# A 14th weight unit in the ring of an expert layer, with one buffer of turned rows and one-hot lists of two experts

## The chip, the cores and the metric

The kernel runs on one core of a Trainium2 chip. Its time is the device time of one execution in microseconds (us). The shapes are fixed: 512 tokens of width 1024, two layers, float32 in and out.

## What is computed

Each of the two layers mixes the tokens (three kinds of attention behind one input projection and one output projection) and then sends every token to 2 of 32 experts. The part that matters here is the second:

```python
def hier_moe(x, rg_w, rg_b, re_w, re_b, w_gate, w_up, w_down):
    t = x.reshape(B * S, D)                       # 512 x 1024
    lg = einsum('td,dg->tg', t, rg_w) + rg_b      # 4 groups
    g_star = argmax(lg, -1)                       # the best group
    le = ...                                      # its 8 experts' logits
    top_v, top_i = lax.top_k(le, 2)               # two experts
    gate = ...                                    # their weights
    for g in range(4):
        h = silu(t @ w_gate[g]) * (t @ w_up[g])   # 1024 -> 256, each of 8 experts
        y = y + (h * gate) @ w_down[g]            # 256 -> 1024
    return y

for l in range(2):
    x = layer_norm(ALPHA * x + hybrid_mixer(x, ...))
    x = layer_norm(ALPHA * x + hier_moe(x, ...))
```

An expert's weights (gate, up, down) are 3 x 1024 x 256 float32 numbers, 3 MB; 32 experts make 96 MB in each layer, read once.

## The kernel before

**Experts.** The kernel does two experts at a time: 16 steps `p` in a layer, and each expert has room for 64 tokens, so a step has 128 rows. For step `p` it gathers 128 rows of the normalised tokens from HBM (`fetch`, `gathered`: an indirect DMA on POOL's queue from `xd` into a part of `xroom`), transposes and scales them (`turned`: 8 PE transposes, then ACT and DVE write `xg`), multiplies by gate and up (`experts_up`, 32 matmuls into `S`), applies silu (`experts_mid`), transposes `h` and multiplies by down (`experts_down`, 16 matmuls into `o`), adds the rows' own share (`half_rows` made it: two DVE operations over 128 x 1024) and scatters the result to `y2` with another indirect DMA. `lists(b)` makes the row numbers and weights of four experts, that is of two steps: DVE compares positions with slots (`hots`, the one-hot matrix `oneh`), PE multiplies it with a table of tokens, and a few small DVE operations turn that into row numbers (`slot_rows`). `oneh` has one buffer.

**The ring of weights.** An expert's 3 MB are two units of 128 x 3072 float32 (1536 KB): `u` = 0 holds gate and up for k = 0 to 5, `u` = 1 the rest of them and down. A layer loads 64 units in a fixed order (both experts' `u` = 0, then both experts' `u` = 1). Each goes into the next place of a ring that is written out as a string, one letter a place:

```python
RING = "UUAAARTTXUUmm"
...
EW.setdefault(e, {})[u] = unit(RING[(2 * j + d) % len(RING)], "w")
SP.dma_start(EW[e][u][:, c0:c1], a["w_e"][l, e, u, :, c0:c1])
```

The letters name memory that the attention part uses for something else: U four slots of projection weights, A three work areas, R the landing area of raw weights, X a part of `xroom` (free when the output projection has read its input there), T and m units of the pool that replaces attention's tiles (`moe`). 13 letters make 13 units of room: unit n + 13 can be loaded when unit n has been read for the last time. `load_next(n)` emits n pairs of units: one pair before attention's softmax part, two within the output projection, three when the pool `moe` opens, and then two pairs in every step, one after `experts_up` and one after `experts_down`. Loads are issued by SP, in order; each waits at SP until its room is free. A scheduler at compile time orders each engine's instructions by their place in the program and by when it thinks they are ready, so a load whose room is free earlier can stand in SP's queue ahead of one that was emitted before it.

**The end of a layer.** At step 13 the first half of the result (`yf`) is read back into two units (one m, one A), at the end the second half and the norm's rows (`yt`, two A units). The next layer's first projection weights are loaded through the landing area R (`raw_room`, `load_pair`: SP loads, ACT and DVE or POOL split into two parts).

Of the kernel before, what the change touches and what calls it, by code (L numbers as in the profile page):

```python
# [7 lines left out]
F32 = mybir.dt.float32  # L8
F32R = mybir.dt.float32r
# [3 lines left out]
OP = mybir.AluOpType  # L13
# [3 lines left out]
NT = S // 128  # L17
NK = D // 128
# [6 lines left out]
NE, FH, CAP = 32, 256, 64  # L25
# [39 lines left out]
def trunk(tc, a, out, dbg=None):  # L65
# [4 lines left out]
    with es:  # L70
# [9 lines left out]
        def bank(tag):  # L80
            return ps.tile([128, 512], F32, name=tag, tag=tag)
# [14 lines left out]
        def mm(o, l, r, start, stop):  # L96
            return PE.matmul(o, l, r, start=start, stop=stop, skip_group_check=True)  # L97
# [10 lines left out]
        def cc(name):  # L108
            return cst[:, CO[name][0] - KEPT:CO[name][1] - KEPT]
# [60 lines left out]
        RAW = {}  # L170

        def raw_room():
            RAW[0] = raws.tile([128, UNIT], F32, name="raw", tag="raw")
# [74 lines left out]
        for l in range(DEPTH):  # L248
# [40 lines left out]
            def load(c):  # L289
                if c < 9:  # L290
                    Wc[l, c] = load_pair(w_in_src(l, c), chunks[c][1])
# [12 lines left out]
                return [x[:, i, c0:c1] for i in range(NT)]  # L304


            load(2)
            if l == 0:
                setup()
# [115 lines left out]
            t = bank("T")  # L425
# [84 lines left out]
            def unit(kind, name):  # L510

                if kind == "X":
                    return xroom[:, 0:UNIT]
                pool, tag, bufs = dict(U=(slots, "U", 4), A=(ums, "Um", 3), R=(raws, "raw", 1), m=(units["m"], "m", 2), T=(units["m"], "T", 2))[kind]
                return pool.tile([128, UNIT], F32, name=name, tag=tag, bufs=bufs)

            RING = "UUAAARTTXUUmm"

            def load_next(n=1):

# [495 lines left out]

            def turned(xr):

                xg = mo.tile([128, NK, 128], F32, name="xg", tag="xg", bufs=2)
                for h in range(2):  # L1020
                    t = bank("acc")
                    for j in range(4):
                        k = 4 * h + j
                        PE.transpose(t[:, 128 * j:128 * j + 128], xr[:, 128 * k:128 * k + 128], ident)  # L1024
                    for j in range(4):
                        k, o = 4 * h + j, t[:, 128 * j:128 * j + 128]
                        if h:
                            A.activation(xg[:, k], o, AF.Identity, scale=lv[:, 0, k, 0:1], bias=lv[:, 0, k, 1:2])  # L1028
                        else:
                            V.tensor_scalar(xg[:, k], o, lv[:, 0, k, 0:1], lv[:, 0, k, 1:2], op0=OP.mult, op1=OP.add)  # L1030
                return xg
# [43 lines left out]

            RI, XR, XG, HR = {}, {}, {}, {}

            def hots(b):
                P = cp.tile([128, NT, 4, CAP], F32R, name="oneh", tag="oneh")
                for i in range(NT):  # L1080
                    last_on["hot"] = V.tensor_tensor(P[:, i], posm[:, i, 4 * b:4 * b + 4].unsqueeze(2).to_broadcast([128, 4, CAP]),
                                    cc("slot")[:, 0:CAP].unsqueeze(1).to_broadcast([128, 4, CAP]), OP.is_equal)
                return P

            def lists(b, P=None):

                Pf = (P or hots(b)).rearrange("p t e s -> p t (e s)")
                for q in range(2):
                    t = bank("T")
                    e0 = 4 * b + 2 * q  # L1090
                    for i in range(NT):
                        mm(t[:, 0:6], Pf[:, i, 128 * q:128 * q + 128], tok[:, i, :, e0:e0 + 2], i == 0, i == NT - 1)
                    rv = small.tile([128, 3], F32, name="rv", tag="rv", bufs=8)
                    V.tensor_copy(rv[0:64], t[0:64, 0:6:2])
                    V.tensor_copy(rv[64:128], t[64:128, 1:6:2])
                    RI[2 * b + q] = slot_rows(rv)
# [30 lines left out]
            attn.__exit__(None, None, None)  # L1127
            moe = tc.tile_pool(name=f"moe{l}", bufs=1, reuse_waits="tile")
            mo = units["m"] = moe.__enter__()
            load_next(3)  # L1130
            XG[0], HR[0] = turned(XR[0]), half_rows(XR.pop(0))
            lists(1)
            fetch(2)
# [29 lines left out]
            def overflow():  # L1163

                n_items = nc.values_load(eidi[0:1, MAX_ITEMS:MAX_ITEMS + 1], min_val=0, max_val=MAX_ITEMS)
                with tc.For_i(0, n_items) as item:
# [43 lines left out]
                    t = bank("acc")  # L1210
                    for k in range(NK):
                        PE.transpose(t[:, 64 * k:64 * k + 64], xr[0:64, 128 * k:128 * k + 128], ident[0:64, 0:64])
                    xg = mo.tile([128, NK, CAP], F32, name="xg", tag="xg", bufs=2)
                    gb = [lv[:, 0, :, b:b + 1].to_broadcast([128, NK, CAP]) for b in range(2)]
                    V.tensor_tensor(xg, t.rearrange("p (k s) -> p k s", k=NK), gb[0], OP.mult)
                    V.tensor_tensor(xg, xg, gb[1], OP.add)
# [23 lines left out]
            for p in range(NE // 2):  # L1240
# [15 lines left out]
                sts.append(st)  # L1256
                if p == NE // 2 - 3:

                    for j, u in enumerate((unit("m", "yf"), unit("A", "yf"))):
                        yf = carve(u, 0, [2, D])  # L1260
                        for i in range(2):
                            yfs.append(yf[:, i])
                            r = 256 * j + 128 * i
                            firsts.append(SP.dma_start(yf[:, i], y2[r:r + 128, :]))
# [7 lines left out]
                SP.dma_start(gb2[j], a["ln_rows"][l:l + 1, 1, j].to_broadcast([128, D]))  # L1272
            with tc.issue_after(last_on["PE"].ins), tc.issue_after(last_on["V"].ins), tc.issue_after(st.ins):
                if not last:
                    raw_room()
                    Wc[l + 1, 0] = load_pair(w_in_src(l + 1, 0), chunks[0][1], "VG")
            overflow()

# [107 lines left out]
```

## Time and profile before

| | |
|---|---|
| time, median of 3 runs | 1354.07 us (1353.26 to 1357.51) |
| the profiled execution | 1356.09 us, span 1354.3 us |
| mean granted clock of TensorE | 0.948 |
| PE busy | 1172.7 us (87%) |
| DVE busy | 794.8 us (59%) |
| q1 (SP's loads), share of 16 DMA engines | 53.6% of the span |
| HBM read | 282.26 MB |

The span is the time from the first to the last instruction. PE is TensorE (PEld its weight loads), DVE VectorE, ACT ScalarE, POOL GpSimd, and SP the engine that issues most of the DMAs (SPq is its queue of instructions, POOLq and ACTq those of POOL and ACT). L530 is line 530 of the kernel above. A busy share is an average over stages with different limits. In the two expert stages (from about 405 to 637 us and from about 1059 to 1289 us) the weights come from HBM. DMA is the mean busy share of 16 DMA engines.

### The profile page before, as it was taken

What the parts mean: (1) busy time and instruction counts of PE and PEld (TensorE: products, weight loads), DVE (VectorE), ACT (ScalarE), POOL (GpSimd) and SP (SyncE); (2) the same over time, 40 slices, a digit from 0 to 9 for tenths busy, and PEclk for the clock granted to TensorE, in tenths of its full rate; (3) what the DMA queues carried; (4) which work ended last, traced back from release to release, by engine and by line L of the source; (5) the groups of instructions that cost most, each with busy time, mean ns of one, the idle gap of its engine ahead of it and who ended that gap; (6) DMA issues with size and microseconds to landing.
All of it is one profiled execution on the core that took longest, in us unless ns stands there. A gap on an engine that the chain in (4) does not pass through costs nothing. (4 is left out here: it accounts for less than half of the span.)

```text
span 1354.3 us, 18414 instructions
## 1 busy us (share of the span) xinstructions
PE 1172.7 (87%) x6708; PEld 819.8 (61%) x6708; DVE 794.8 (59%) x2007; ACT 424.7 (31%) x1019; POOL 301.4 (22%) x310
## 2 busy tenths in 40 slices
PE   6989999999969999777599899999998799988830
PEld 6989986668944444232498899666697343333310
DVE  6599638675355745332768992667635465533336
ACT  3462247574112111111236322857711111111100
POOL 5322431300111211100542434230011121111013
PEclk9999999999979999989699999899999799999975
DMA  6452440005188999999542524200335899999933
GB/s 237 115 182 82 125 171 12 22 15 218 63 366 321 424 422 423 425 407 339 194 145 74 198 75 135 104 23 23 131 135 235 317 422 424 423 425 420 392 138 125
DMA packets 68317, 302.21 MB, mean 223 GB/s; under 512 B 16128, under 2 KB 20736, under 8 KB 52864
## 3 DMA queue, kind: packets, MB, share of 16 engines
q1 hardware_dynamic: 57696, 280.02, 53.6%
q0 software_dynamic: 9376, 16.80, 3.3%
q10 hardware_dynamic: 1152, 4.19, 0.8%
q8 instruction: 54, 0.88, 0.3%
q14 instruction: 39, 0.32, 0.1%
HBM read 282.26 MB, written 36.01 MB: 235 GB/s over the span
## 5 line engine op out<-in xcount | busy, mean ns | idle before, releaser
L97 PE MATMUL acc<-U,xh 128*128 128x384 f32 (+1 forms) x1584 | 297.7, 342 | 17.4 <-ACT U L196 7.2
L97 PE MATMUL S<-w,xg 128*64 128x512 f32 (+1 forms) x968 | 265.4, 601 | 31.0 <-DMA w<-w_e 18.5
L97 PEld LDWEIGHTS acc<-U,xh 128*128 128x128 f32 x1584 | 279.8, 193 | 20.2 <-ACT U L196 7.4
L97 PEld LDWEIGHTS S<-w,xg 128*64 128x64 f32 x968 | 88.4, 140 | 155.1 <-issue 103.0
L97 PE MATMUL o<-w,hT 128*64 128x512 f32 x488 | 124.7, 597 | 8.3 <-DVE hT L92 4.4
L199 POOL TENSOR_TENSOR U<-raw,U 128x768 fp32r<-128x768 f32 (+2 forms) x46 | 92.2, 2010 | 176.1 <-ACT U L196 169.3
L1057 ACT ACTIVATE h<-S 128x256 f32<-128x256 f32 x32 | 12.3, 384 | 357.1 <-PE S L97 357.1
L1058 DVE TENSOR_TENSOR h<-h,S 128x256 f32<-128x256 f32 x32 | 13.4, 420 | 175.2 <-ACT h L1057 175.1
L1013 POOL DMA_INDIRECT xroom<-xd,ri x33 | 40.7, 1232 | 261.2 <-issue 193.3
L196 ACT ACTIVATE U<-raw 128x768 fp32r<-128x768 f32 (+2 forms) x88 | 68.2, 812 | 83.0 <-PE acc L97 42.0
L97 PEld LDWEIGHTS o<-w,hT 128*64 128x64 f32 x488 | 40.8, 136 | 72.0 <-issue 49.9
L199 DVE TENSOR_TENSOR U<-raw,U 128x768 fp32r<-128x768 f32 (+2 forms) x42 | 51.5, 1227 | 42.1 <-ACT U L196 39.5
L1072 DVE SCALAR_TENSOR_TENSOR xroom<-o,rv,xroom 128x512 f32<-128x512 f32 x64 | 47.8, 750 | 42.7 <-PE o L97 39.5
L1073 POOL DMA_INDIRECT y<-xroom,ri x32 | 32.7, 1022 | 170.3 <-DVE xroom L1072 146.5
L1028 ACT ACTIVATE xg<-acc,lv 128x128 f32<-128x128 f32 x128 | 48.1, 456 | 57.1 <-PE acc L1024 55.9
L90 ACT ACTIVATE uc<-T 128x512 f32<-128x512 f32 (+3 forms) x117 | 51.4, 461 | 40.6 <-PE T L297 38.5
L97 PE MATMUL acc<-U,oh 128*128 128x384 f32 (+1 forms) x384 | 63.3, 315 | 0.0
L97 PEld LDWEIGHTS acc<-U,oh 128*128 128x128 f32 x384 | 56.8, 189 | 1.2 <-issue 1.0
L1024 PEld LDWEIGHTS acc<-cst,xroom 128*128 128x128 f32 x256 | 29.7, 149 | 38.2 <-issue 25.9
L1036 DVE TENSOR_TENSOR xroom<-xroom,gb 128x1024 f32<-128x1024 f32 (+1 forms) x33 | 40.2, 1219 | 20.1 <-DMA xroom<-xd,ri 20.0
L403 DVE MATCH_REPLACE8 uc<-m,uc 128x256 f32<-128x256 f32 (+2 forms) x96 | 51.4, 540 | 0.0
L1030 DVE TENSOR_SCALAR xg<-acc,lv 128x128 f32<-128x128 f32 x128 | 43.6, 402 | 12.6 <-PE acc L1024 12.6
(377 smaller groups left out, 2034.5 us busy)
## 6 DMA issues: line engine op xcount, KB each, us to landing
w<-w_e SPq DMA_DIRECT2D x110, 1536.0 KB, 26.0
raw<-w_in SPq DMA_DIRECT2D x64, 384.0 KB, 3.6
xroom<-w_e SPq DMA_DIRECT2D x8, 1536.0 KB, 25.8
w<-w_e SPq DMA_DIRECT2D x24, 512.0 KB, 15.1
y<-uc SPq DMA_DIRECT2D x2, 4096.0 KB, 14.2
raw<-w_o SPq DMA_DIRECT2D x16, 384.0 KB, 3.5
xd<-yn ACTq DMA_DIRECT2D x8, 512.0 KB, 6.8
yf<-y SPq DMA_DIRECT2D x8, 512.0 KB, 11.2
```

The source lines that it names most:

```text
L90: A.activation(o, i, AF.Copy, scale=1.0 if scale is None else scale)
L97: return PE.matmul(o, l, r, start=start, stop=stop, skip_group_check=True)
L196: A.activation(hi, r, AF.Copy)
L199: e.tensor_tensor(lo, r, hi.bitcast(F32), OP.subtract)
L403: V.match_replace(out=acc_t[i][:, :n], in_to_replace=m8, in_values=acc_t[i][:, :n], imm_value=TAKEN)
L1013: G.indirect_dma_start(out=xr[0:n], out_offset=None, in_=xd, in_offset=bass.IndirectOffsetOnAxis(ap=ri[0:n], axis=0), bounds_check=S - 1, ...
L1024: PE.transpose(t[:, 128 * j:128 * j + 128], xr[:, 128 * k:128 * k + 128], ident)
L1028: A.activation(xg[:, k], o, AF.Identity, scale=lv[:, 0, k, 0:1], bias=lv[:, 0, k, 1:2])
L1030: V.tensor_scalar(xg[:, k], o, lv[:, 0, k, 0:1], lv[:, 0, k, 1:2], op0=OP.mult, op1=OP.add)
L1036: V.tensor_tensor(y[0:n], xr[0:n], gb1[0:n, 0], OP.mult)
L1072: last_on["V"] = V.scalar_tensor_tensor(y[:, c], o[n], rows[1], y[:, c], op0=OP.mult, op1=OP.add)
L1073: return G.indirect_dma_start(out=y2, out_offset=bass.IndirectOffsetOnAxis(ap=rows[2], axis=0), in_=y, in_offset=None, bounds_check=2 * S ...
```

## The change

A 14th place in the ring, a third `m` unit, and the units in another order: X and one U now come ahead of T T, three m behind them, and a U stands last. Four pairs instead of three are emitted when `moe` opens, so that 14 units are emitted ahead of step 0 instead of 12. For the room, `xg` has one buffer instead of two, and `oneh` holds two experts instead of four: `hots` is called twice in `lists`, with one buffer, so its second call must wait until PE has read the first. `yf` goes into two m units, and the next layer's first raw weights into an m unit instead of R; R is taken again when the next layer loads its third piece (`load(2)`).

```diff
@@ -304,6 +304,8 @@
                 return [x[:, i, c0:c1] for i in range(NT)]
 
 
+            if l:
+                raw_room()
             load(2)
             if l == 0:
                 setup()
@@ -511,10 +513,10 @@
 
                 if kind == "X":
                     return xroom[:, 0:UNIT]
-                pool, tag, bufs = dict(U=(slots, "U", 4), A=(ums, "Um", 3), R=(raws, "raw", 1), m=(units["m"], "m", 2), T=(units["m"], "T", 2))[kind]
+                pool, tag, bufs = dict(U=(slots, "U", 4), A=(ums, "Um", 3), R=(raws, "raw", 1), m=(units["m"], "m", 3), T=(units["m"], "T", 2))[kind]
                 return pool.tile([128, UNIT], F32, name=name, tag=tag, bufs=bufs)
 
-            RING = "UUAAARTTXUUmm"
+            RING = "UUAAARXUTTmmmU"
 
             def load_next(n=1):
 
@@ -1016,7 +1018,7 @@
 
             def turned(xr):
 
-                xg = mo.tile([128, NK, 128], F32, name="xg", tag="xg", bufs=2)
+                xg = mo.tile([128, NK, 128], F32, name="xg", tag="xg", bufs=1)
                 for h in range(2):
                     t = bank("acc")
                     for j in range(4):
@@ -1075,21 +1077,21 @@
 
             RI, XR, XG, HR = {}, {}, {}, {}
 
-            def hots(b):
-                P = cp.tile([128, NT, 4, CAP], F32R, name="oneh", tag="oneh")
+            def hots(p):
+                P = cp.tile([128, NT, 2, CAP], F32R, name="oneh", tag="oneh")
                 for i in range(NT):
-                    last_on["hot"] = V.tensor_tensor(P[:, i], posm[:, i, 4 * b:4 * b + 4].unsqueeze(2).to_broadcast([128, 4, CAP]),
-                                    cc("slot")[:, 0:CAP].unsqueeze(1).to_broadcast([128, 4, CAP]), OP.is_equal)
+                    last_on["hot"] = V.tensor_tensor(P[:, i], posm[:, i, 2 * p:2 * p + 2].unsqueeze(2).to_broadcast([128, 2, CAP]),
+                                    cc("slot")[:, 0:CAP].unsqueeze(1).to_broadcast([128, 2, CAP]), OP.is_equal)
                 return P
 
             def lists(b, P=None):
 
-                Pf = (P or hots(b)).rearrange("p t e s -> p t (e s)")
                 for q in range(2):
+                    Pf = (hots(2 * b + q) if q or P is None else P).rearrange("p t e s -> p t (e s)")
                     t = bank("T")
                     e0 = 4 * b + 2 * q
                     for i in range(NT):
-                        mm(t[:, 0:6], Pf[:, i, 128 * q:128 * q + 128], tok[:, i, :, e0:e0 + 2], i == 0, i == NT - 1)
+                        mm(t[:, 0:6], Pf[:, i], tok[:, i, :, e0:e0 + 2], i == 0, i == NT - 1)
                     rv = small.tile([128, 3], F32, name="rv", tag="rv", bufs=8)
                     V.tensor_copy(rv[0:64], t[0:64, 0:6:2])
                     V.tensor_copy(rv[64:128], t[64:128, 1:6:2])
@@ -1127,7 +1129,7 @@
             attn.__exit__(None, None, None)
             moe = tc.tile_pool(name=f"moe{l}", bufs=1, reuse_waits="tile")
             mo = units["m"] = moe.__enter__()
-            load_next(3)
+            load_next(4)
             XG[0], HR[0] = turned(XR[0]), half_rows(XR.pop(0))
             lists(1)
             fetch(2)
@@ -1210,7 +1212,7 @@
                     t = bank("acc")
                     for k in range(NK):
                         PE.transpose(t[:, 64 * k:64 * k + 64], xr[0:64, 128 * k:128 * k + 128], ident[0:64, 0:64])
-                    xg = mo.tile([128, NK, CAP], F32, name="xg", tag="xg", bufs=2)
+                    xg = mo.tile([128, NK, CAP], F32, name="xg", tag="xg", bufs=1)
                     gb = [lv[:, 0, :, b:b + 1].to_broadcast([128, NK, CAP]) for b in range(2)]
                     V.tensor_tensor(xg, t.rearrange("p (k s) -> p k s", k=NK), gb[0], OP.mult)
                     V.tensor_tensor(xg, xg, gb[1], OP.add)
@@ -1256,7 +1258,7 @@
                 sts.append(st)
                 if p == NE // 2 - 3:
 
-                    for j, u in enumerate((unit("m", "yf"), unit("A", "yf"))):
+                    for j, u in enumerate((unit("m", "yf"), unit("m", "yf"))):
                         yf = carve(u, 0, [2, D])
                         for i in range(2):
                             yfs.append(yf[:, i])
@@ -1272,7 +1274,7 @@
                 SP.dma_start(gb2[j], a["ln_rows"][l:l + 1, 1, j].to_broadcast([128, D]))
             with tc.issue_after(last_on["PE"].ins), tc.issue_after(last_on["V"].ins), tc.issue_after(st.ins):
                 if not last:
-                    raw_room()
+                    RAW[0] = unit("m", "raw")
                     Wc[l + 1, 0] = load_pair(w_in_src(l + 1, 0), chunks[0][1], "VG")
             overflow()
```

## Rows read from the trace of the kernel before

**Rows 1.** Page, part 2: GB/s moved in 40 slices of the span.

```profile
GB/s 237 115 182 82 125 171 12 22 15 218 63 366 321 424 422 423 425 407 339 194 145 74 198 75 135 104 23 23 131 135 235 317 422 424 423 425 420 392 138 125
```

**Rows 2.** Chain that ended last, layer 2: start us, us, what.

```profile
1126.61 32.08 DMA w<-w_e
...
1259.25 0.61 PE S L97
```

**Rows 3.** Windows: length, busy of PE, PEld, DVE, ACT, POOL, clock, DMA share, GB/s.

```profile
406.00:416.00 10.00, 10.00 (x52) 4.42 (x52) 3.98 (x11) 3.91 (x9) 0.98 (x1) 0.91 0.54 184
...
420.00:424.00 4.00, 4.00 (x22) 1.35 (x20) 3.14 (x7) 0.00 (x0) 1.17 (x1) 1.00 0.61 223
424.00:604.00 180.00, 161.39 (x752) 70.39 (x749) 84.48 (x229) 24.56 (x67) 27.99 (x25) 0.99 1.01 420
...
1062.00:1070.00 8.00, 8.00 (x40) 2.96 (x36) 1.46 (x5) 1.89 (x3) 0.00 (x0) 0.93 0.50 162
...
1076.00:1082.00 6.00, 6.00 (x28) 1.85 (x24) 2.45 (x5) 0.00 (x0) 1.48 (x2) 1.00 0.54 167
1082.00:1260.00 178.00, 160.93 (x751) 65.42 (x751) 87.67 (x236) 26.45 (x72) 27.68 (x24) 0.99 1.01 421
```

**Rows 4.** DMA issues: times, KB each, median us from issue to landing.

```profile
w<-w_e SPq DMA_DIRECT2D x110, 1536.0 KB, 26.0
...
xroom<-xd,ri POOLq DMA_INDIRECT x33, 9.8
```

**Rows 5.** Timeline of SP, layer 2 (start us, us, what), and its longest waits.

```profile
1031.41 0.33 SPq L530 DMA_DIRECT2D w<-w_e  x1
...
1048.03 0.80 SPq L530 DMA_DIRECT2D w<-w_e  x2
1067.35 0.81 SPq L530 DMA_DIRECT2D w<-w_e  x2
1078.82 2.08 SPq L530 DMA_DIRECT2D w<-w_e  x4
...
SPq L530 <- DMA xd<-yn: 21.6, 2, 13.1
```

**Rows 6.** Timeline of PE, first step of layer 2.

```profile
1060.83 8.21 PE L97 MATMUL S<-w,xg 128*64 128x512 f32 x32
1068.97 1.09 PE L1024 MATMUL acc<-cst,xroom 128*128 128x128 f32 x8
...
1075.19 3.60 PE L97 MATMUL o<-w,hT 128*64 128x512 f32 x16
```

**Rows 7.** Waits of PE, 1126 to 1262 us, then 460 to 640 us.

```profile
PE S L97 <- DMA w<-w_e: 9.3, 5, 2.9
...
PE S L97 <- DMA w<-w_e: 9.2, 5, 3.2
```

**Rows 8.** Timeline of DVE and POOL ahead of the first gather.

```profile
1037.84 0.29 DVE L941 TENSOR_TENSOR sel<-Lg,ghot 128x128 f32<-128x128 f32 x1
...
1041.28 1.46 DVE L1081 TENSOR_TENSOR oneh<-posm,cst 128x256 fp32r<-128x256 f32 x4
...
394.35 1.37 POOL L1013 DMA_INDIRECT xroom<-xd,ri  x1 [6.03 <-DVE ri L995]
...
1049.17 1.23 POOL L1013 DMA_INDIRECT xroom<-xd,ri  x1 [6.16 <-DVE oneh L1081]
```

**Rows 9.** Timelines of PE and DVE: list products and half rows, layer 2.

```profile
1045.45 1.29 PE L97 MATMUL T<-tok,oneh 128*128 128x6 f32 x8 [3.02 <-DVE tok L1123]
...
1058.69 1.23 DVE L1036 TENSOR_TENSOR xroom<-xroom,gb 128x1024 f32<-128x1024 f32 x1 [6.37 <-DMA xroom<-xd,ri]
```

**Rows 10.** Timelines of PE, ACT and DVE at the end of layer 1.

```profile
620.83 3.65 PE L97 MATMUL o<-w,hT 128*64 128x512 f32 x16 [1.59 <-ACT hT L90]
...
642.18 1.48 ACT L196 ACTIVATE U<-raw 128x656 fp32r<-128x656 f32 x2 [10.39 <-DMA raw<-w_in]
...
647.07 1.61 DVE L199 TENSOR_TENSOR U<-raw,U 128x656 fp32r<-128x656 f32 x1 [0.52 <-ACT U L196]
```

## The prediction

> **What bounds the kernel now.** I began with the page's 40 slices: each expert stage has five slices at 407 to 425 GB/s in a row, and none outside these stages comes near [rows 1]. The chain that ended last tells the same of layer 2: it runs over the landing of weights from 1126.61 us on, and PE's last wait for a weight ends at 1259.25 [rows 2]. So in the body of an expert stage the stream of weights sets the time, and PE, though busy nine tenths of it, waits for them: 9.3 us in layer 2; in layer 1 9.2, waits for the unit in `xroom` aside [rows 7].
>
> A stream that never pauses can only be made shorter by starting earlier or by closing pauses, so next I took windows. In layer 1 the 16 DMA engines are at 1.01 from 424 to 604 us, in layer 2 from 1082 to 1260; but just ahead of that the share falls twice: to 0.54 in 406 to 416 and 0.61 in 420 to 424, and to 0.50 in 1062 to 1070 and 0.54 in 1076 to 1082 [rows 3]. Idle DMA time is 10 x 0.46 + 4 x 0.39 = 6.2 us in layer 1 and 8 x 0.50 + 6 x 0.46 = 6.8 us in layer 2. SP's timeline says why: loads go out from 1031.41, the last two of the 13 units at 1048.03, then nothing until 1067.35, when step 0 has read its first two units, and again nothing until 1078.82 [rows 5]. PE's timeline has the other side: the 32 matmuls of the first `experts_up` take 1060.83 to 1069.04, and `experts_down` is through at 1078.79 [rows 6]. The ring is full, and the stream stands until PE gives room back.
>
> **The change part by part.**
>
> *The 14th place.* A unit is 1536 KB [rows 4], 1.573 MB; at the 421 GB/s of the body [rows 3] that is 3.73 us. With 14 places, whatever is waited for, the stream is one unit further each time that the same room comes free. The order of releases stays: before, the loads at 1078.82 were units 15 to 18, now they are 16 to 19. So the stream ends 3.73 us earlier, if the first pause can take that much: it is 4.0 us in layer 2 and 4.6 in layer 1, so it can, barely, and the second pause stays. Behind the last pause DMA is never idle until the end of the body, so nothing gives it back there. On PE's side the gain arrives if PE could have been 3.73 us earlier at its last wait: from step 0 on its own work plus its waits for weights fill the time, and the waits to be had are 9.3 us and at least 9.2 [rows 7], both over 3.73. Two layers: 7.5 us. Bounds: 0 (the place isn't filled ahead) and 7.5.
>
> *The order of the places.* X and a U in front of T T: nothing. The loads behind the output projection began at 1031.41 already, so SP's queue had what is free first in front, whatever the string says; the two last, for the m units, went out at 1048.03, when the normalised rows had landed in HBM (SP's longest such wait is 13.1 us) [rows 5]. Five units go out by then, or four if SP holds the last U behind the m's: 4 x 3.73 = 14.9 us of transfer from about 1033 on, and the rows' own writes beside it, against a wait until 1048. The cover is thus within some 1 us; without it the stream stands for at most about that.
>
> *One `xg`.* ACT and DVE may write the next `xg` only when `experts_up` has read the old one. The transposes for the next step stand behind that `experts_up` on PE anyhow, at 1068.97 behind 1060.83 to 1069.04 [rows 6], and `xg` is written from their result. Cost nothing; the cover is PE's order.
>
> *`oneh` of two experts.* Each call of four DVE operations over 128x256 (1.46 us for four) becomes two calls of four over 128x128. The nearest row of that shape and kind takes 0.29 [rows 8]; the step between two such operations lies between half of 1.46 / 4 and all of it, 0.18 to 0.37. With 8 calls a layer DVE has 8 x (8 x 0.18 to 0.37 less 1.46), 0 to 12 us more work, taken as 8 x (8 x 0.25 - 1.46) = 4.3. It has the room: busy 84.5 of 180 us in the body [rows 3], so 0 on the path there. The Trainium skill (VectorE: DVE Perf Modes, The TRN2 errata) says that VectorE pays a fixed cost for each instruction, so that many small ones pay it many times, and would speak against this edit; by its formula, 58 cycles plus one an element at 0.96 GHz, I estimate 8 x 8 x 0.194 - 8 x 4 x 0.327 = 1.9 us more a layer. No run here shows that split, and the sum is the same by either.
>
> What counts is the head of the stage. There `hots` stands ahead of the first gather. The first call is now four half operations, 0.29 against 0.42 each, and only one set of four products stands ahead of the first list's copies, where eight took 1.29 [rows 9]. I take 0.8 us earlier (0.5 from DVE, 0.3 from copies of the second list that came between; bounds 0 and 1.5). In layer 1 the first gather at 394.35 waited for the row numbers [rows 8], so it moves, with it PE's start, each release, and the stream's second pause. In layer 2 the gather at 1049.17 [rows 8] comes just after the rows landed at 1048 [rows 5], and stays. I take 0.6 us in all.
>
> The second call must wait for PE, and its four products wait for it: four operations at 0.25, half of 1.29 for the products [rows 9] and the hand-overs, some 2 us longer in line for the second list. Its row numbers serve the second gather, which step 1 needs some 9 us after the first, so this is hidden. If DVE stands in `half_rows` then, 2 x 1.23 us [rows 9] come on top, and PE, in order, could stand with it: that is a rival.
>
> *`yf` and the raw weights.* The yt units are now read until `experts_down` of step 14, which is through at 624.5, well ahead of the end; `yf` in m units of step 13: nothing. The raw weights of layer 2 land at 642.18 in layer 1's tail [rows 10]; an m unit of step 13 is free before R of step 14 was. If SP therefore issues them sooner, the splits leave DVE's way, 1.61 us at 647.07 [rows 10] and as much again shared with POOL. I take 0, bounds 0 and -2.5.
>
> **Sum.** 7.5 + 0.6 = 8.1 us. The profiled execution took 1356.09 with its span of 1354.3, 2.0 over the median of 1354.07; the terms are differences within that span, and I take them off the median: 1346.0.
>
> **Rivals.** About what a measurement here can tell from no change is 0.3%, 4.06 us.
>
> *A list stalls PE, mildly.* If PE's order puts the second products of a list ahead of `experts_up` or `experts_down` of step 0, and DVE has them behind `half_rows`, PE stands for `half_rows` and the four one-hots, 2.46 + 1.0, 3.4 us in each layer, and every later release moves with it. Against it: list products stand spread among the matmuls, and DVE made its one-hots long ahead. 1346.0 + 6.8 = 1352.8, no change. Chance 0.12.
>
> *The same at two lists or more in both layers* ends on the other side: with 0.65 for the products and 0.3 for hand-overs a list is 4.4, two are 8.8 a layer, less 3.7: 1354.1 + 2 x 5.1 = 1364. It decides from 5.8 us of stall a layer on (3.7 plus half of 4.06). Only lists ahead of step 2 can do it, since later the stream has a lead. Chance 0.05.
>
> *The gathers come later.* If a gather had to wait for all weights queued before it, a 14th unit would cost each 3.73 us, PE's start would move by that, and nothing be won: 1354. Against it: a gather lands 9.8 us after its issue while a load of weights takes 26.0 [rows 4], the transfer time of seven units, so it passes most of what is queued ahead of it. Chance 0.04.
>
> *The 14th unit isn't loaded ahead* because the third m unit's room lies where attention's last tiles are, or SP's order holds it: only the gain at the head and some of one layer is left, 1352. Chance 0.06.
>
> *The raw weights come sooner* and the layer boundary shrinks by 2.5: 1343.5. Chance 0.11.
>
> **How the numbers follow.** The forecast, both pauses shortened by a unit and no stall, has 0.62; its own range is 1343.5 to 1349.5, from the bounds of the head (0 to 1.5 a layer), of the last U (1 a layer) and 1 for a different order of instructions elsewhere. The 80% range takes in the boundary and most of the mild stall: 1341.5 to 1352.0. Faster by over 0.3% (under 1350.0) holds the forecast, the boundary, and little else: 0.76. Slower is the second rival: 0.05. The rest, 0.19, is no change.
>
> **What would show it.** SP issues 14 units before the pause, at 1048 three or four instead of two; the first window of low DMA share shrinks to almost nothing, by about 3.7 us of idle time in each layer, while the second stays; the body keeps 420 GB/s; PE's waits for weights in the body fall little, and shift. Right for the lists: DVE busy some 8 us more in all and no idle time of PE that `oneh` ends, beyond 2 us. Wrong: a first `experts_up` later than now after the first gather, idle time in the body of the stream, or a first pause as long as before.

## Result and the profile after

The changed kernel takes 1348.99 us (median of 15 runs, 1342.81 to 1352.79), the kernel before, run in turn with it, 1356.19 us (15 runs, 1353.26 to 1358.72): ratio 0.9941, 95% interval 0.9931 to 0.9952, or 8.0 us less (6.5 to 9.4); the two medians themselves differ by 7.2 us. Forecast were 8.1 us less and 1346.0 us; the absolute number is 3.0 us off mainly because the kernel before came out 2.1 us above the median that the forecast started from.

Windows of the changed kernel over the stretches of [rows 3], moved with the stage (columns as there):

```profile
406.00:416.00 10.00, 10.00 (x45) 4.00 (x45) 3.82 (x17) 3.32 (x7) 0.99 (x1) 0.84 0.93 359
422.00:426.00 4.00, 4.00 (x22) 1.34 (x20) 2.14 (x6) 0.00 (x0) 1.22 (x2) 1.00 0.58 137
424.00:604.00 180.00, 165.64 (x774) 76.31 (x772) 90.79 (x258) 26.18 (x71) 27.85 (x25) 0.99 1.00 417
...
1060.00:1066.00 6.00, 6.00 (x36) 2.81 (x34) 1.22 (x4) 1.19 (x4) 0.00 (x0) 1.00 0.80 286
1070.00:1076.00 6.00, 6.00 (x30) 2.01 (x28) 3.82 (x13) 0.00 (x0) 1.62 (x2) 1.00 0.53 167
1076.00:1250.00 174.00, 160.03 (x752) 65.55 (x748) 87.17 (x252) 25.64 (x70) 27.72 (x25) 1.00 1.01 421
```

Before, the DMA engines stood 6.2 us in layer 1 and 6.8 us in layer 2. Now it is 10 x 0.07 + 4 x 0.42 = 2.4 us and 6 x 0.20 + 6 x 0.47 = 4.0 us. Nearly all that went is the first pause (4.6 to 0.7, 4.0 to 1.2 us); the second stays (1.6 and 1.7, 2.8 and 2.8). The rest of the stage runs at 417 and 421 GB/s, as before.

SP's timeline of the changed kernel in layer 2, to be laid beside [rows 5]:

```profile
1027.37 0.33 SPq L532 DMA_DIRECT2D xroom<-w_e  x1
...
1043.23 1.75 SPq L532 DMA_DIRECT2D w<-w_e  x4
1062.40 0.80 SPq L532 DMA_DIRECT2D w<-w_e  x2
1074.21 2.37 SPq L532 DMA_DIRECT2D w<-w_e  x4
```

When the normalised rows have landed, four units go out where two went (one of them, for the last U, had gone out before that wait in the kernel before), then two when `experts_up` has read the first pair, then four after `experts_down`. PE's timeline (first three lines) and its waits (us in total, times, longest; layer 1, 460 to 640 us; then layer 2, 1120 to 1255 us), against [rows 6, 7]:

```profile
1056.28 7.81 PE L97 MATMUL S<-w,xg 128*64 128x512 f32 x32
1064.02 1.09 PE L1026 MATMUL acc<-cst,xroom 128*128 128x128 f32 x8
1070.57 3.60 PE L97 MATMUL o<-w,hT 128*64 128x512 f32 x16
```

```profile
PE S L97 <- DMA w<-w_e: 5.8, 4, 2.9
PE S L97 <- DMA xroom<-w_e: 1.1, 1, 1.1
PE T L97 <- DVE oneh L1083: 0.3, 1, 0.3
...
PE S L97 <- DMA w<-w_e: 5.4, 3, 2.7
PE S L97 <- DMA xroom<-w_e: 1.6, 1, 1.6
```

In layer 2 the waits for weights fell from 9.3 to 7.0 us. `oneh` ends 0.3 us of PE's idle time. Around step 0, from 404 to 426 and from 1054 to 1078 us, PE's only wait is the one for the first gathered rows (6.4 and 8.4 us). DVE's group for `oneh` (busy us, mean ns of one, idle us before) and the first gather of each layer on POOL (against [rows 8]):

```profile
L1083 DVE TENSOR_TENSOR oneh<-posm,cst 128x128 fp32r<-128x128 f32 x128 | 33.2, 285 | 0.7
```

```profile
394.42 1.32 POOL L1015 DMA_INDIRECT xroom<-xd,ri  x1 [5.24 <-DVE rv L1097]
...
1044.35 1.16 POOL L1015 DMA_INDIRECT xroom<-xd,ri  x1 [7.08 <-PE T L97]
```

Before, the same group was 64 operations of 419 ns, 24.5 us.

**Where the time went, by stage.** I read four marks in each layer off the timelines: the first `oneh`, the start of the first `experts_up`, the end of the last `experts_down`, the first load of `yt` from `y2`. In us, layer 1 / layer 2:

| | first `oneh` to `experts_up` | first `experts_up` to last `experts_down` | from there to `yt` |
|---|---|---|---|
| before | 19.9 / 19.6 | 230.4 / 227.8 | 9.6 / 32.4 |
| after | 18.4 / 20.5 | 226.3 / 223.9 | 10.8 / 32.3 |
| difference | -1.5 / +0.9 | -4.1 / -3.9 | +1.2 / -0.1 |

Below, head, body and tail stand for the three columns. The differences sum to -7.5 us; the rest of the two profiled spans (1354.3 and 1345.1) differs in stretches with the same work, such as from layer 1's first load of `yt` to layer 2's first load into `xroom`, which took between 384.1 and 386.7 us over all kernels profiled here.

### The profile page after: what moved, and what is told of

It reads as the page before. It is cut to its first block, busy times and chain, and to the rows that moved or that the text cites. A ratio compares the mean times of both kernels' runs of the same rounds, so it can differ in the third digit from the quotient of the medians.

```text
span 1345.1 us, 18497 instructions
## 1 busy us (share of the span) xinstructions
PE 1168.4 (87%) x6701; PEld 822.8 (61%) x6708; DVE 800.2 (59%) x2071; ACT 424.7 (32%) x1019; POOL 298.0 (22%) x310
## 5 line engine op out<-in xcount | busy, mean ns | idle before, releaser
L97 PEld LDWEIGHTS acc<-U,xh 128*128 128x128 f32 x1584 | 276.4, 191 | 22.7 <-ACT U L196 7.5
L97 PE MATMUL S<-w,xg 128*64 128x512 f32 (+1 forms) x984 | 263.2, 599 | 24.6 <-DMA w<-w_e 11.2
L97 PEld LDWEIGHTS S<-w,xg 128*64 128x64 f32 x984 | 93.4, 140 | 146.2 <-issue 100.9
L1075 POOL DMA_INDIRECT y<-xroom,ri x32 | 32.3, 1010 | 167.2 <-DVE xroom L1074 135.6
## 6 DMA issues: line engine op xcount, KB each, us to landing
w<-w_e SPq DMA_DIRECT2D x18, 512.0 KB, 18.5
y<-uc SPq DMA_DIRECT2D x2, 4096.0 KB, 14.3
w<-w_e SPq DMA_DIRECT2D x8, 768.0 KB, 14.4
xd<-yn ACTq DMA_DIRECT2D x8, 512.0 KB, 11.7
```

The lines of the kernel that those rows point to most:

```text
L1075: return G.indirect_dma_start(out=y2, out_offset=bass.IndirectOffsetOnAxis(ap=rows[2], axis=0), in_=y, in_offset=None, bounds_check=2 * S ...
```

## Experiments

Two theories stood against each other from the start. **Lead**: the gain is one unit of transfer a layer, because one more unit is in SBUF when the ring is full and the stream stands. **Other parts**: the lists, the single `xg`, the order or the raw weights bring it. A third, **room**, came up later: a deeper ring helps throughout the body, not just at its start. (In the later expectations on 13 and 12 places, on the lists and on the late places these are theory A, rival C and rival B; the other expectations say what theirs are.) Each kernel was timed against the kernel before.

**13 places again, first try.** The changed kernel with two m units and one m place fewer:

```
-            RING = "UUAAARXUTTmmmU"
+            RING = "UUAAARXUTTmmU"
-            load_next(4)
+            load_next(3)
```

with `yf` in an m and an A unit and the raw weights in R, as before.

> The changed kernel with 13 places again (UUAAARXUTTmmU, two m units, three pairs ahead of step 0, yf and the raw weights placed as before); the new order, the single xg and the halved one-hot lists stay. If the 14th place makes the gain (3.73 us a layer), this stands within 3 us of the kernel before: ratio 0.998 to 1.001, and the first pause of the stream is back at 4 us and more of idle DMA time a layer. If the order of the places or the lists make it, it stays near 0.994.

Measured: 1366.53 us, ratio 1.0067 (1.0045 to 1.0089). The body is back at 230.2 and 227.6 us, as the lead has it, but the whole is slower than the kernel before. SP's timeline of this kernel after layer 1, and PE's wait there:

```profile
621.80 13.56 SPq L1264 DMA_DIRECT2D yf<-y  x4
635.40 0.91 SPq L1272 DMA_DIRECT2D yt<-ln_rows  x2
636.35 3.74 SPq L194 DMA_DIRECT2D raw<-w_in  x4
```

```profile
PE o L97 <- DMA raw<-w_in: 15.7, 1, 15.7
```

In this order an m place holds a unit that the last step still reads, and it is the one that `yf` gets. SP stands at `yf`, and the norm's rows and the raw weights behind it wait too: from the last `experts_down` to `yt` it takes 15.6 us instead of 9.6. The run mixes two things, so I made it again.

**13 places, with `yf` in units that are free early.** The ring is "UUAAARXUTTUmm"; the rest as above.

> The changed kernel with 13 places again (two m units, the last place of the order left out; yf and the raw weights where the kernel before has them, so that no tail load waits for a late unit). Theory A (the gain is the lead: one unit of transfer a layer, loaded before the pause): from the first experts_up to the last experts_down 230.2 us in layer 1 and 227.6 in layer 2, as with the 13 places tried first and as in the kernel before, the pauses back at full length, the tail after layer 1 within 10.8 us and that of layer 2 near 32.4, so 1353.0 to 1356.5 us, ratio 0.997 to 1.001. Rival C (lists, single xg or order bring the gain): ratio 0.994 to 0.996 with 226 and 224 us.

Measured: 1357.37 us, ratio 1.0004 (0.9995 to 1.0013). Body 231.3 and 228.0 us, tail of layer 1 9.4 us. Without the 14th place, the new order, the lists and the single `xg` together are worth nothing that can be measured.

**Lists and single `xg` alone.** The kernel before with

```
-                xg = mo.tile([128, NK, 128], F32, name="xg", tag="xg", bufs=2)
+                xg = mo.tile([128, NK, 128], F32, name="xg", tag="xg", bufs=1)
...
+            def hots(p):
+                P = cp.tile([128, NT, 2, CAP], F32R, name="oneh", tag="oneh")
```

> The kernel before with the single xg and the one-hot lists of two experts alone; ring, order, yf and raw weights as before. Theory A: body 230.4 and 227.8 us (within 0.6), the head of layer 1 shorter by 0.5 to 1.5 us, that of layer 2 by 0 to 0.5, DVE busy 5 to 9 us more; 1354.5 to 1356.5 us, ratio 0.9985 to 1.0005. Rival C: ratio 0.994 to 0.997. Rival D (the lists cost PE something that the 14th place more than pays): ratio above 1.002.

Measured: 1357.78 us, ratio 1.0009 (1.0000 to 1.0018); body 231.5 and 228.2. From the first `oneh` to the first `experts_up` it is 18.5 us in layer 1, where the kernel before has 19.9, and 19.5 in layer 2, where it has 19.6. So the head of layer 1 is 1.4 us shorter in this profile; in the total it doesn't show.

**Old order, 14 places.** RING = "UUAAARTTXUUmmm".

> 14 places in the old order (UUAAARTTXUUmmm), all else as in the changed kernel. If only the number of places counts, ratio 0.993 to 0.995 as with the change. If X and U ahead of T T matter, because loads would stand behind T T in SP's queue, it loses 2 us or more: 0.996 or higher.

Measured: 1350.84 us, ratio 0.9955 (0.9940 to 0.9971), body 226.2 and 224.3. **Raw weights in R**, the other parts as changed:

```
-                    RAW[0] = unit("m", "raw")
+                    raw_room()
```

> The changed kernel with the next layer's first raw weights landing in R again and no second taking of R for the third piece. The theory of the prediction prices this at nothing: ratio 0.993 to 0.995. The rival, that the shorter stretch between the layers (2.1 us more won from the read-back of y to the end of layer 2's output projection) comes from the raw weights, expects 1.5 to 2.5 us less gain: 0.9955 to 0.996.

Measured: 1349.47 us, ratio 0.9948 (0.9929 to 0.9967), body 226.0 and 223.8. Neither can be told from the changed kernel. The forecast's rival that the raw weights would shorten the layer boundary by 2.5 us falls.

**12 places.** RING = "UURAAAXTTUUm", one m unit, `yf` in two A units, `yt` in an A and a U unit.

> The changed kernel with 12 places (one m unit; order U U R A A A X T T U U m; yf in two A units, yt in an A and a U unit, so that they are free early). Theory A: another unit of lead less, 3.7 us a layer over 13 places: first experts_up to last experts_down 234 us in layer 1 and 231.3 in layer 2, first pause 7.5 us longer than with 14; 1361 to 1364 us, ratio 1.003 to 1.006. Rival B (a deeper ring helps the body as such, with less and less for each place): a step from 12 to 13 well over 5 us a layer, ratio above 1.008; or under 1.5 us a layer, ratio under 1.000.

Measured: 1366.53 us, ratio 1.0076 (1.0063 to 1.0090). The body, 234.2 and 231.4 us, is what the lead said. The ratio is 0.0016, 2.2 us, above the upper end of what was expected; the two stretches to `yt`, whose units were laid out in another way here, took 11.7 and 33.7 us, 3.6 more than the 9.4 and 32.4 with 13 places.

**14 places, two of them loaded late.** First by an order given to the scheduler:

```
+                with (tc.issue_after(last_on["up"].ins) if p == 0 else ExitStack()):
+                    load_next(2 if p == 0 else 1)
```

> The changed kernel with all its 14 places, but the units for the last two places are issued only when the first experts_up is through: 12 units of lead, and a ring of 14 from there on. Theory A: the first pause 7.5 us longer, and the second, 1.7 us of idle DMA in layer 1 and 2.8 in layer 2, gone since four units go out at the first release; so the body 226.3 + 7.5 - 1.7 = 232.1 us in layer 1 and 223.9 + 7.5 - 2.8 = 228.6 in layer 2, 10.5 us in all: 1359.5 us, ratio 1.0024 (1.000 to 1.004). Rival B (what counts is the room in the ring, not when its last places are first filled): 1349 us, ratio 0.994 to 0.997.

Measured: 1348.78 us, ratio 0.9944 (0.9932 to 0.9957). SP's timeline of this kernel says why this decides nothing:

```profile
1044.32 1.75 SPq L532 DMA_DIRECT2D w<-w_e  x4
```

All four units still went out when the rows had landed; the order is one of the program, not a wait on the chip. The run is a repeat of the changed kernel. The second try writes one element a row of the two units from the result of the first `experts_up`, so that their loads depend on it:

```
+                        if after is not None:
+                            V.tensor_copy(EW[e][u][:, 0:1], after)
...
+                if p == 0:
+                    load_next(1, gu[:, 0:1])
```

> The changed kernel with all its 14 places, but each of the units for the last two places is first written, one element a row, with a value from the result of the first experts_up, so that their loads must wait for that result: 12 units of lead and a ring of 14 from there on. (The hold by issue order tried before moved nothing: SP sent the loads as early as before.) Theory A (lead): the first pause 7.5 us longer, the second, 1.7 us of idle DMA in layer 1 and 2.8 in layer 2, gone; body 226.3 + 7.5 - 1.7 = 232.1 us and 223.9 + 7.5 - 2.8 = 228.6 us: 1359.5 us, ratio 1.0024 (1.000 to 1.004). Rival B (room): 1349 us, ratio 0.994 to 0.997.

Measured: 1362.30 us, ratio 1.0039 (1.0026 to 1.0053). SP's timeline and the windows of this kernel in layer 2:

```profile
1049.46 0.80 SPq L534 DMA_DIRECT2D w<-w_e  x2
...
1072.53 2.12 SPq L534 DMA_DIRECT2D w<-w_e  x4
```

```profile
1060.00:1076.00 16.00, 15.06 (x64) 6.89 (x64) 8.43 (x36) 4.57 (x10) 0.98 (x1) 0.77 0.26 80
1076.00:1084.00 8.00, 8.00 (x41) 3.11 (x42) 6.04 (x19) 0.00 (x0) 1.49 (x2) 1.00 1.02 435
```

The two units go out with the next two at 1072.53, the stream stands for 16 x 0.74 = 11.8 us, and the second pause is gone. Body 232.3 us (232.1 expected) and 230.8 us (228.6 expected; 1.4 us of the excess are the first `experts_up`, which takes 9.24 us at a granted clock still low, against 7.81). A ring of 14 places that is filled late is worse than one of 13 filled early. Room alone is not the gain; the lead is.

**What is left of the pauses: PE's order.** The second pause ends with the first `experts_down`, and PE does a part of step 1's `experts_up` ahead of that. I turned it round:

```
-                gu = experts_up(XG.pop(p), w)
+                with (tc.issue_after(last_on["PE"].ins) if p == 1 else ExitStack()):
+                    gu = experts_up(XG.pop(p), w)
```

> The changed kernel, but on PE the gate and up matmuls of step 1 stand behind the down matmuls of step 0, so that the second units of step 0 come free some 3 us earlier and the stream's second pause closes; PE has 7 us of waits for weights left in each layer to pay for its idle time. If pauses of the stream set the time, 1 to 2.8 us a layer are won: ratio 0.990 to 0.9925. If PE had no room left, or the second pause costs nothing, 0.994 or higher.

Measured: 1350.58 us, ratio 0.9955 (0.9938 to 0.9973), no gain. PE's timeline of this kernel up to layer 2's `experts_down`, and three windows over its start (the last three numbers are granted clock, DMA share and GB/s):

```profile
1069.74 0.24 PE L97 MATMUL T<-tok,oneh 128*128 128x6 f32 x1 [1.73 <-DVE rr L993]
...
1071.10 5.15 PE L97 MATMUL o<-w,hT 128*64 128x512 f32 x16
```

```profile
1068.00:1070.00 2.00, 0.27 (x3) 0.29 (x3) 1.96 (x13) 1.25 (x4) 0.00 (x0) 1.00 1.00 424
1070.00:1072.00 2.00, 1.79 (x7) 0.93 (x8) 1.92 (x9) 0.00 (x0) 0.00 (x0) 0.69 1.04 442
1072.00:1074.00 2.00, 2.00 (x8) 0.71 (x6) 2.00 (x8) 0.00 (x0) 0.68 (x1) 0.50 0.94 399
```

PE has little to do here, 0.27 us of work in the first of these windows: DVE is busy 1.96 of these 2 us with `xg`, `h` and a list, and the transposes of `h` stand on PE behind products of that list, for which PE waits 1.73 us. The granted clock, 1.00 from 1060 to 1250 us in the changed kernel, falls to 0.50 (1.2 GHz), and the 16 matmuls take 5.15 us instead of 3.60. What the order won in layer 2, the clock took: `experts_down` starts 12.4 us after the first `experts_up` does, instead of 14.3, and ends after 17.6, instead of 17.9. In layer 1 the body is even longer, 227.9 us against 226.3: there the 16 matmuls, with others between them, take from 418.08 to 424.64. So I put 14 matmuls of no use into that gap:

```
+                if p == 0:
+                    with tc.issue_after(last_on["up"].ins):
+                        warm(14)
```

> As the try with experts_down of step 0 ahead of step 1's experts_up, and 14 matmuls of no use between the first experts_up and that experts_down, so that PE is not idle there. Theory A: granted clock stays 1.00, the 16 matmuls of experts_down take 3.6 us and not 5.15, end 2 us earlier than in the changed kernel, and the second pause shortens by up to 1.7 us in layer 1 and 2.5 in layer 2, while PE loses 3 us of its 7 us of waits: ratio 0.9915 to 0.9945. Rival: the work put off costs PE as much as the pause gives: 0.9945 to 0.9965.

Measured: 1355.50 us, ratio 0.9993 (0.9984 to 1.0002), worse than either theory had it. PE's timeline of the try before (first line) and of this kernel, layer 1:

```profile
418.08 1.30 PE L97 MATMUL o<-w,hT 128*64 128x512 f32 x2 [0.37 <-ACT hT L90]
...
413.79 3.19 PE L97 MATMUL o<-bfc 128*128 128x512 bf16 x14
...
419.53 0.24 PE L97 MATMUL T<-tok,oneh 128*128 128x6 f32 x1 [1.33 <-DVE rr L993]
...
420.55 1.07 PE L97 MATMUL o<-w,hT 128*64 128x512 f32 x2 [0.37 <-ACT hT L90]
```

The 14 matmuls run ahead of the transposes for step 1 and of the list, and push these back; the transposes of `h` stand behind the list's products, which wait for DVE, as in the try before. So `experts_down` starts at 420.55 where that try had 418.08, no earlier than the 420.37 of the changed kernel, while the matmuls of step 1 that PE did in that time are still to do. In layer 2 the granted clock fell even so, to 0.57 over 1074 to 1078 us, and the 16 matmuls took 5.35 us. What the idea is worth at a full clock was not measured.

**What is left of the pauses: loads in parts.** Each place becomes one tile that all its units share, so that a load waits only for the readers of what it overwrites, and the four units that go out after the pause are loaded in parts:

```
+                    cuts = {7: (0, 1536, UNIT), 8: (0, 1024, 2048, UNIT)}.get(j, cuts)
...
+                        i = (2 * j + d) % len(RING)
+                        if i not in places:
+                            places[i] = unit(RING[i], "w")
+                        EW.setdefault(e, {})[u] = places[i]
```

> The changed kernel; each of the 14 places is one tile that its units share, so that a load has to wait only for the readers of what it overwrites, and the first four units that go out after the pause are loaded in parts (two halves for the first pair, three parts of 1024, 1024 and 1024 columns for the second). Theory A: what is left of the pauses, 0.7 + 1.7 us of idle DMA in layer 1 and 1.2 + 2.8 in layer 2, closes to under 1 us a layer, and PE's remaining waits for weights (7 us a layer) let the end move with it: body 224 to 225.5 us in layer 1, 220.5 to 222 in layer 2; 4 to 6 us under the changed kernel, 1343 to 1345 us, ratio 0.9900 to 0.9920. If the pauses are no longer what limits, or the loads wait for whole units all the same: 0.9935 to 0.9955.

Measured: 1344.40 us, ratio 0.9916 (0.9902 to 0.9930), as expected. It is the fastest kernel of this study, about 3.4 us (0.9941 less 0.9916) under the changed kernel; that step goes through the kernel before, since the two were not run side by side. One tile for each place and the parts were not tried apart. SP's timeline and windows of this kernel in layer 2:

```profile
1057.49 5.09 SPq L537 DMA_DIRECT2D w<-w_e  x6
1070.17 3.75 SPq L537 DMA_DIRECT2D w<-w_e  x6
```

```profile
1056.00:1068.00 12.00, 12.00 (x64) 5.11 (x62) 6.35 (x34) 2.33 (x6) 0.41 (x1) 1.00 1.01 410
1068.00:1076.00 8.00, 8.00 (x39) 2.93 (x36) 3.77 (x10) 0.38 (x1) 1.59 (x2) 1.00 0.94 330
```

The first parts go out 3.7 us after the first `experts_up` begins instead of 6.1, and the idle time of 4.0 us is 8 x 0.06 = 0.5. Body 225.0 and 222.0 us, 1.3 and 1.9 less than the changed kernel; so in layer 2 the body gave back about half of the idle time that closed. In layer 1 the tail is shorter too, and up to `yt` the gain is 2.3 us. Of this, 1.0 is the first `experts_up` (7.63 us against 8.61, at a mean granted clock of 0.87 against 0.78 over 404 to 416 us); 1.3 is left for places and parts.

**The same with 13 places**, on the kernel before, to see whether parts can replace the place (cuts for j = 6, 7 and 8):

> The kernel before with its 13 places, its double xg and its lists of four experts; only each place is one tile that its units share, and the first loads after the pause go in parts (two halves; three parts of 1024 columns for the next two pairs); yf in a U and an A unit, so that it is free early. Theory A (idle time of the stream just after the ring fills is what the stage loses, however it is closed): two thirds of the two units that waited for experts_down, 2 x 2/3 x 3.73 = 5.0 us of transfer, can go before it, half of that from the end of experts_up on, and the first halves some 3 us earlier; 2.5 to 4.3 us of the 6.2 and 6.8 us of idle DMA close, body 226.5 to 228.5 us in layer 1 and 224 to 226 in layer 2, ratio 0.9945 to 0.9970 without a 14th place. Rival (it takes a whole unit of room more): 0.9985 to 1.0010.

Measured: 1356.33 us, ratio 0.9993 (0.9981 to 1.0005); body 231.1 and 227.9 us: a miss. SP's timeline of this kernel in layer 2:

```profile
1048.82 0.81 SPq L535 DMA_DIRECT2D w<-w_e  x2
1065.20 5.09 SPq L535 DMA_DIRECT2D w<-w_e  x6
```

With an odd number of places, the first pair that was cut has one unit for the last free place. Its parts are issued in turn with those of the unit that must wait, so half of a unit that could have been loaded at once stood behind a waiting load from 1048.82 to 1065.20. Whether 13 places gain once that pair is left whole was not tried.

**All in one table.** The trace's list of queues gives the MB that SP's queue had moved from the start of the program to a moment. I took the end of the first `experts_down`, and the time from there to the end of the last; layer 1 / layer 2. The rows of the queue for the changed kernel, to 423.97 and 1074.18 us (packets, MB, share):

```profile
q1 hardware_dynamic: 18912, 56.88, 38.2%
...
q1 hardware_dynamic: 46752, 194.03, 48.2%
```

| kernel | MB moved by then | us from there to the last `experts_down` |
|---|---|---|
| 12 places | 53.74 / 190.88 | 216.3 / 213.5 |
| 14, two held | 53.71 / 191.24 | 214.7 / 211.5 |
| before (13) | 55.31 / 192.46 | 213.9 / 209.9 |
| 13 places, second try | 55.31 / 192.46 | 213.5 / 209.7 |
| 13 in parts | 55.35 / 192.55 | 213.1 / 209.8 |
| changed (14) | 56.88 / 194.03 | 208.5 / 206.0 |
| 14 in parts | 57.62 / 195.14 | 208.1 / 203.9 |

A place is 1.57 MB, one unit, within 0.01. From 12 to 13 to 14 places, that unit takes 2.4 to 2.8 and 5.0 to 5.4 us off the rest of layer 1, 3.6 to 3.8 and 3.7 to 3.9 off layer 2, where 3.73 was forecast each time. The first try with 13 places, with the same 55.31 MB, has 212.6 us in layer 1: 3.7 under 12 places, 4.1 over 14. The kernel in 13 parts moved no more than the one before, and won nothing. The held one is better than its MB say; it has no second pause, which would fit, but that was not tried apart.

## Why the prediction was right

**The 14th place** carried the sum, as forecast: 3.73 us a layer, against a body shorter by 4.1 and 3.9 us in the two profiles. Over four kernels with 13 places (before, the two tries, the lists alone) the body is 230.9 / 227.9 us in the mean, over four with 14 (changed, old order, raw in R, the hold that held nothing) 226.2 / 224.1: 4.7 and 3.8 us. Shown: the two late places of the held kernel and the 12 places move the body by what the lead gives. Layer 1's surplus of about 1 us over one unit does not reach the end of the layer: from the first `experts_up` to `yt` it is 240.6 us in the mean with 13 places (before, second try, lists alone) and 237.0 with 14 (the same four), 3.6 us. Where it goes stands under the last point below.

**The pauses** did what was said: first almost gone, second unchanged, 14 units issued before the pause. In layer 2 the idle time fell by 2.8 us, less than the 3.7 of the forecast, though the whole 1.57 MB more had been moved.

**PE's waits for weights** were to fall little, and that was wrong: in layer 2 from 9.3 to 7.0 us, in layer 1 from 9.2, and 3.2 for the unit in `xroom` besides, to 5.8 and 1.1. PE's work is nearly the same in both kernels, so at an equal clock a shorter body can only come out of PE's idle time. The forecast used this in the term itself, as the waits "to be had", and forgot it in the list of signs.

**The head** came out at 0.6 us, the number forecast, by two errors that cancel: layer 1 gained 1.5 where 0.8 was taken (the bound was 1.5), and layer 2, put at 0, lost 0.9. How much of the gain the lists bring is less sure than the two profiles make it look: from the first `oneh` to `experts_up` of layer 1, the kernels with the new lists took 17.9 to 18.5 us, the two with the old ones 19.9 (before) and 18.7 (13 in parts). Of the loss in layer 2, 0.7 lies between the first `oneh` and the gather: 7.8 to 7.9 us in the three kernels with the old ring (before, lists alone, 13 in parts), 8.1 to 8.6 in all with another one, of 12, 13 or 14 places. So it goes with the ring. In the chain of the changed kernel the last normalised rows take 11.75 us to land:

```profile
1031.33 11.75 DMA xd<-yn
1044.35 9.76 DMA xroom<-xd,ri
```

In the three kernels with the old ring the same rows land 11.0 to 11.2 us after their issue, in the others 11.7 to 11.8 wherever the trace has it. More weights issued ahead of them are not the reason: the second try with 13 places has 11.74 and the 12 places 11.79, with as many loads ahead of these rows as in the kernel before, and the changed kernel has one fewer. The cause stays open.

**Lists and `xg`.** `oneh` costs DVE 33.2 - 24.5 = 8.7 us in both layers (8.6 forecast); in all, DVE's busy time rose by 5.4 us, to 800.2, where some 8 were forecast. The row has 285 ns for one operation and 0.92 us for four in line, a step of 0.23 us, where 0.25 was taken. The Trainium skill's fixed cost (VectorE: DVE Perf Modes, The TRN2 errata) is seen: half the elements take 285 of 419 ns, not half. Of the two formulas in that section, the one that the forecast took gives 194 and 327, both some 90 ns under the rows; by the other, 151 cycles plus one an element, stated for an fp32 `tensor_tensor` add, I estimate 291 and 424, as the rows have it within 6 ns. The rivals in which a list stalls PE fall: `oneh` ends 0.3 us of idle time, and the 5.0 us that end with `rr`, in six waits for a list's products, lie ahead of the first gathered rows. The mechanism does exist: in both tries with `experts_down` ahead, a list's products held PE for 1.73 and 1.33 us in step 0.

**Order, `yf`, raw weights** at nothing: right by the runs above for order and raw weights. SP did hold the last U behind the m's, and the stream did not stand for it (DMA share 0.98 to 1.03 from 1028 to 1048 us). For `yf` the forecast was right, and the first try with 13 places shows that it was not a matter of course: 6.0 us of layer 1's tail hang on which unit `yf` gets.

**Missed: what ends layer 1.** From the last `experts_down` to `yt`, layer 1's tail, 1.2 us seem lost: 9.4 to 9.6 us with 13 places in four kernels (the first try aside), 10.6 to 10.8 in seven with 14, yet 9.8 with 14 in parts. But `yt` doesn't wait for that `experts_down`. SP's timeline and ACT's last wait for the raw weights, before and after:

```profile
621.25 0.33 SPq L530 DMA_DIRECT2D w<-w_e  x1
646.29 1.39 ACT L196 ACTIVATE U<-raw 128x656 fp32r<-128x656 f32 x2 [2.63 <-DMA raw<-w_in]
646.55 2.29 SPq L1292 DMA_DIRECT2D yt<-y  x5
...
617.95 0.33 SPq L532 DMA_DIRECT2D w<-w_e  x1
642.95 1.39 ACT L196 ACTIVATE U<-raw 128x656 fp32r<-128x656 f32 x2 [1.36 <-DMA raw<-w_in]
643.20 3.45 SPq L1294 DMA_DIRECT2D yt<-y  x5
```

From the layer's last load of weights (first line of each) to `yt` it takes 25.2 to 25.5 us in twelve kernels (30.3 in the first try with 13 places, 26.2 with 12, where `yf` or the norm's rows wait for other units), and `yt` goes out just after the raw weights have landed, 1.3 and 3.0 us after the last step's scatter has. In R or in an m unit, the raw weights go out 11.3 us after that last load, so the choice changes nothing. Only PE's end moves against this: the last `experts_down` ends 15.6 to 16.0 us after that last load in five kernels (before, second try, lists alone, 13 in parts, 14 in parts) and 14.4 to 14.7 in the nine others. In these five the granted clock falls to 0.50 for 3.4 to 6.8 us within the last 40 us of the body; in the nine it is 1.00 there. The first 10 of these 40 us, before and after (granted clock, DMA share and GB/s stand last):

```profile
597.00:607.00 10.00, 6.85 (x18) 2.94 (x18) 2.86 (x7) 1.70 (x5) 0.00 (x0) 0.66 0.96 387
...
592.40:602.40 10.00, 7.26 (x34) 3.29 (x32) 3.28 (x8) 1.89 (x5) 0.69 (x1) 1.00 0.97 396
```

So some 1.2 us are body in one kernel and tail in the other, and up to `yt` they cost nothing: that is both layer 1's surplus and the loss in its tail. That the clock makes them is likely, since the two go together in all fourteen kernels; no run changed it alone.

## What to carry to other kernels

Where a ring of buffers feeds a stream that sets the time, count the stream's idle time just after the ring first fills, not the buffers: another buffer is worth one buffer's transfer as long as that pause lasts, and only if it is filled before the pause. When no room is left for one, let the first loads after the pause wait for parts of a buffer, but (from one failed try, not from a mended one) keep loads that may go ahead of those that must wait, for SP issues its loads in order. Before taking memory that a later stage uses, see which unit is read last there.

## What the runs showed of the hardware

In one place a short idle time of PE cost about as much again. In layer 2 of the try with `experts_down` first, PE was busy 0.27 of the 2 us from 1068 on, the granted clock of the next 4 us was 0.69 and 0.50, and the next 16 matmuls took 1.55 us longer than in the changed kernel. The first `experts_up` of a stage, after some 5.5 to 9 us in which PE waits for the gather, took between 7.63 and 9.24 us over the kernels here for the same 32 matmuls, so a difference of 1 us in a stage's first step means little by itself.
